# The two S5 recurrences of a four-layer trunk in a written order on all engines

## The chip, the cores and the metric

The kernel runs on one core of a Trainium2 chip. Its time is the device time of one execution in microseconds; several executions give a median. A profile is one execution, taken by the hardware profiler. The core has five engines with instruction queues of their own, which run side by side and meet through semaphores: PE (TensorE, matrix products and transposes; PEld is its weight load), DVE (VectorE), ACT (ScalarE), POOL (GpSimd) and SP (SyncE, which here only issues DMAs). Each of them takes its instructions in the order of its queue, so that an instruction that waits holds up all that stand behind it.

## The reference, cut to what matters

A trunk of four layers on 512 positions of width 1024. Layers 0 and 3 mix by an S5 recurrence, layer 1 by gated linear attention, layer 2 by differential attention; each is followed by a SwiGLU FFN. The change touches the S5 layers only:

```python
def s5_mixer(h, lam_re, lam_im, log_dt, b_re, b_im, c_re, c_im, d_skip, w_glu):   # h = rmsnorm(x, norm_mix[layer])
    dt = jnp.exp(log_dt)[:, None]
    ab = exp((lam_re + 1j * lam_im) * dt)             # 64 groups of 64 states (written as re, im in the reference)
    bb = (ab - 1) / lam * b                           # 64 groups, 64 states, 16 inputs
    for chunk in chunks(h, 64):                       # u: positions x 64 groups x 16
        bu = einsum('bcgh,gph->bcgp', u, bb)
        s = associative_scan(s_t = ab * s_(t-1) + bu_t), started from the chunk before
        y = real(einsum('bcgp,ghp->bcgh', s, c))
    y = y + d_skip * h
    z = gelu(y)
    a, b = split(z @ w_glu, 2)
    return a * sigmoid(b)
...
x = x + mix;  h = rmsnorm(x, norm_ffn[layer]);  x = x + swiglu_ffn(h, w_gate_up[layer], w_down[layer])
```

## The kernel before, in words

**The whole.** `Trunk.run` goes through `s5_first` (layer 0), an FFN, `gla`, an FFN, `diff`, an FFN, `s5_second` (layer 3), an FFN and the last norm. Products of weights are made in three passes over a high and a low half of each operand (`mm3`, lines 368 to 372): ScalarE casts the high half (L346), VectorE subtracts it for the low half (L350). Weights arrive in `wst` tiles (three buffers) and are split into `whl` tiles (five buffers).

**The order of work.** By default a list scheduler orders each engine's instructions by priorities and its own costs. `self.hand(engines)` ends the part before and opens one in which the named engines take their instructions as they are written (`hand_all` for all five; `hand()` goes back to the scheduler). The first blocks of each FFN, the attention and parts of `gla` are written like that; before the change, both S5 layers are left to the scheduler. `issue_after` puts the instructions of a block behind one of another place, on that one's engine.

**One S5 layer.** Four positions are taken together: a step of the recurrence goes over 128 blocks of four positions. `s5_pipe` (L1266) works through eight steps `kk`, each for 8 of the 64 groups (128 channels):

- `up`: four transposes turn `hu` (the normed input) into U, one of four buffers of `room` (L1290, copied by ScalarE L1303; for the first four steps of the second layer VectorE scales them, L1299).
- `states`: 8 products with the input operator `in` into two PSUM banks `V` (L1311); VectorE multiplies by cosine and sine `cs` (L1313 to L1316) and adds the pairs (L1318, L1319), on GpSimd in layer 0, on VectorE in layer 3.
- `scans`: two scans with the decays `r4` (L1328, L1330) and four products that turn back, into `prods` (L1329, L1331 to L1333).
- `outputs`: 20 products with the operators `map` and `out` into `y` (L1340, L1342), then Gelu on ScalarE (L1344).
- `turned`: four transposes `zp` (L1353), and the high (L488) and low (L489) halves of `zT`.
- `glu`: 12 three-pass products of 512 columns with `w_glu`'s second half, over steps into four banks `acc`, which `s5_glu` reads through Tanh (L1548).

A turn of the loop at L1374 writes `states(kk)`, `scans(kk-1)`, `up(kk+1)`, the `steps` hook, `outputs(kk-2)`, `turned(kk-2)` and `glu(kk-3)`. The two pairs of `mods` and `prods` hold four of the five `whl` buffers while the recurrence runs, so one is left for the halves of `w_glu`.

**Where the operators come from.** In layer 0 they are made while it runs. `s5_small` makes the parameters, `s5_x` the input operators X of eight blocks (parts `one` and `two`, by `cross`, L1017 to L1019, on VectorE), `s5_xt` and `s5_inm` turn them into `in` (L1143, four ScalarE copies L1153), `s5_q` makes the output operators Q (base copies L1075, `cross` on GpSimd), `s5_out_pads` and `s5_b_pads` lay them out by DMA on SP, `s5_rows` and `s5_map` make `map` (L1110, L1120, a trip through DRAM). `s5_phases_first` makes cosines and sines of a step: rough turns (L987 to L992, banks `tp`), their fraction (L994 to L996), a clip on VectorE (L998) and three ScalarE operations (L999 to L1001), where sine and Gelu need different function tables; then the decays (L1003, L1004). The `steps` hook makes them for `kk + 1`. The input is normed by `s5_in` over `normed` (L470 to L484): squares on ScalarE, the power on GpSimd, scaling and the norm's weight on ScalarE and GpSimd for two of four quarters and on VectorE for the others.

In layer 3 the operators were made under earlier FFNs and lie in DRAM; `steps` loads them one step ahead (L1505, L1513), with the decays' copy (L1516) on ScalarE.

Of the kernel before, what the change touches and what calls it, by code (L numbers as in the profile page):

```python
# [11 lines left out]
F32 = mybir.dt.float32  # L12
# [256 lines left out]
class Trunk:  # L269
# [558 lines left out]
    def sincos(self, pool, sn, cs, r, n, tag):  # L828
# [6 lines left out]
        with self.tc.high_priority(offset=60):  # L835
            nc.scalar.activation(sn, r, AF.Sin)
            nc.scalar.activation(cs, a[:], AF.Sin, scale=-1.0, bias=self.halfpi[:])


    def s5_small(self, pool):  # L840
# [6 lines left out]
        nc.scalar.activation(warm[:], self.halfpi[:], AF.Sin)  # L847
        self.magic = cp.tile([P, 1], F32, name="magic")
# [5 lines left out]
        if True:  # L854
# [5 lines left out]
            draw = p.tile([16, P], F32, name="draw")  # L860
            nc.sync.dma_start(draw[:], i["s5_d"].rearrange("l (k p) -> (l k) p", p=P))
# [6 lines left out]
            nc.tensor.transpose(ps[:, 3, :16], draw[:], self.ident[:16, :16])  # L868
# [10 lines left out]
            v.tensor_copy(self.dcol[:], ps[:, 3, :16])  # L879
# [58 lines left out]
        p = Slices(self.wp.tile([P, 2048], F32, tag="whl", name="params2", bufs=5))  # L938
        self.s5_rows_of_phases(p, pool, keep["fhi"], keep["flo"], keep["f"])
# [3 lines left out]
    def s5_rows_of_phases(self, p, cp, fhi, flo, f):  # L943
# [4 lines left out]
        v = nc.vector  # L948
        part = p.tile([P, 96], F32, name="rowparts").rearrange("p (k z b) -> p k z b", z=3, b=4)
# [8 lines left out]
        v.tensor_tensor(lo, lo, rest, op=ALU.subtract)  # L958
# [19 lines left out]
    def s5_phases_first(self, pool, kk, cs, r4):  # L978


        nc = self.nc
        mm = nc.tensor.matmul
        flat = lambda y: y[:].rearrange("p a b -> p (a b)")
        row = self.frow[:, kk]
        fine, rest = (self.counts[:, z].rearrange("p a b -> p (a b)") for z in range(2))
        rough = flat(self.tp("rough"))
        mm(rough, row, fine, start=True, stop=False)  # L987
        mm(rough, row, rest, start=False, stop=True)
        k = pool.tile([P, 512], F32, tag="turns", name="turns")
        nc.scalar.activation(k[:], rough, AF.Identity, bias=self.magic[:])  # L990
        kr = pool.tile([P, 512], F32R, tag="turnsr", name="turnsr")
        nc.scalar.activation(kr[:], k[:], AF.Identity, bias=self.mmagic[:])  # L992
        g = flat(self.tp("angle"))
        mm(g, row, fine, start=True, stop=False)  # L994
        mm(g, self.nident[:], kr[:], start=False, stop=False)
        mm(g, row, rest, start=False, stop=True)  # L996
        ca = k[:]
        nc.vector.tensor_scalar(ca, g, -0.5, 0.5, op0=ALU.max, op1=ALU.min)  # L998
        nc.scalar.activation(cs[:, 1], ca, AF.Sin, scale=self.two_pi)  # L999
        nc.scalar.activation(ca, ca, AF.Abs)  # L1000
        nc.scalar.activation(cs[:, 0], ca, AF.Sin, scale=-self.two_pi, bias=self.halfpi[:])  # L1001
        r4 = r4.rearrange("p (b m) -> p b m", m=P)
        nc.scalar.copy(r4, self.k5["r4"][:, 4 * kk : 4 * kk + 4].unsqueeze(2).broadcast_to([P, 4, P]))  # L1003
        nc.gpsimd.memset(r4[:, :, 0:1], 0.0)  # L1004
# [28 lines left out]
    def s5_x(self, eng, pool, L, b0, nb, bb, bufs=1):  # L1033
# [4 lines left out]
        def one():  # L1038
            f(0, 0, X[:, 0, :, 0], bb[:, 0], bb[:, 1], ALU.subtract)
# [96 lines left out]

    def s5_xt(self, X, z, b0):
# [11 lines left out]
    def s5_inm(self, dst, ps):  # L1149
        d = dst.rearrange("p (b n) -> p b n", n=P)  # L1150
        for g in range(2):
            r = slice(g * 64, (g + 1) * 64)
            self.nc.scalar.copy(d[r, :, r], ps[r, :, r])  # L1153
# [105 lines left out]
    def s5_in(self, p, l, xin, pool, aside=False):  # L1259
        g = self.gain(self.i["norm_mix"][l])  # L1260
# [932 lines left out]
```

## Time and profile before

| | |
|---|---|
| median of three runs | 2357.49 us (2357.08 to 2360.3) |
| the profiled execution | 2366.1 us, its span 2364.4 us |
| mean granted TensorE clock | 0.977 |
| first scan products (L1313) of layer 0 | 48.6 us from the start |
| gates of layer 0 read (L1548) | from 201.7 us |
| first scan products of layer 3 | 1846.8 us |
| gates of layer 3 read | from 1939.6 us |

The profile gives busy times by engine, the waits with what ended them, and a timeline of instructions (start, duration, engine, line, operation, tiles, times merged; in brackets the idle time before it and its releaser). Durations of pipelined instructions overlap a little, so that the distance from one start to the next is the time one costs. The PEclk column is the granted clock of TensorE as a share of full speed.

### The profile page before, as it was taken

The page shows a single profiled execution, that of the slowest core. Times are in us where ns is not written, and L with a number is a line of the kernel's source. Part 1 is how long each engine was busy: PE and PEld are TensorE (multiplying, and loading weights), DVE is VectorE, ACT ScalarE, POOL GpSimd, SP SyncE. Part 2 cuts the span into 40 slices and gives each one's busy share as a digit, 9 for nine tenths or more (in the row PEclk, how much of TensorE's full clock was granted, in tenths as well). Part 3 has the DMA queues.
Part 4 walks back from the last instruction along what each step waited for, and adds up shares of the span by engine and source line. Part 5 has one row for each costly group of instructions (what it writes and reads, how often), then busy time and mean ns, then how long its engine had stood idle before and what let it go on. Part 6 is the DMA issues. An engine that isn't in the chain of part 4 may idle for free. (4 is left out here: it accounts for less than half of the span.)

```text
span 2364.4 us, 37216 instructions
## 1 busy us (share of the span) xinstructions
PE 2245.8 (95%) x14847; PEld 1985.6 (84%) x14847; DVE 1586.0 (67%) x2416; ACT 1119.2 (47%) x1790; POOL 332.3 (14%) x417
## 2 busy tenths in 40 slices
PE   4799989999999999999999998999999799999997
PEld 3577888898977789898987787989999688989996
DVE  7765587876833468786753566886856864967674
ACT  3454454554552346555544575653534233634442
POOL 3330123324000011111001231111000100101000
PEclk9699999999999999999999999999999899999999
DMA  4114676676332268576344564895742545766631
GB/s 111 32 39 142 160 186 155 165 178 156 86 104 72 79 144 212 146 181 177 108 140 116 115 134 122 209 240 127 187 98 81 121 130 151 176 175 157 162 77 67
DMA packets 291719, 320.17 MB, mean 135 GB/s; under 512 B 68005, under 2 KB 231097, under 8 KB 291290
## 3 DMA queue, kind: packets, MB, share of 16 engines
q1 hardware_dynamic: 229434, 236.57, 33.4%
q0 software_dynamic: 62112, 81.22, 18.7%
q8 instruction: 117, 1.92, 0.3%
q14 instruction: 56, 0.46, 0.1%
HBM read 285.88 MB, written 16.65 MB: 128 GB/s over the span
## 5 line engine op out<-in xcount | busy, mean ns | idle before, releaser
L350 DVE TENSOR_TENSOR whl<-wst,whl 128x1024 fp32r<-128x1024 f32 x272 | 332.1, 1223 | 310.2 <-ACT whl L346 309.6
L346 ACT CAST whl<-wst 128x1024 fp32r<-128x1024 f32 x272 | 285.2, 1050 | 383.2 <-PE acc L372 265.5
L535 PE MATMUL a<-side,whl 128*128 128x256 f32 x3168 | 388.7, 280 | 9.0 <-ACT whl L346 5.9
L535 PEld LDWEIGHTS a<-side,whl 128*128 128x128 f32 x3168 | 375.9, 191 | 11.0 <-ACT whl L346 7.1
L370 PE MATMUL acc<-whl,act 128*128 128x512 f32 x704 | 278.2, 395 | 3.0 <-DVE g L580 3.0
L371 PE MATMUL acc<-whl,act 128*128 128x512 f32 x704 | 275.0, 391 | 0.0
L372 PE MATMUL acc<-whl,act 128*128 128x512 f32 x704 | 274.7, 390 | 0.0
L535 PE MATMUL c<-side,whl 128*128 128x256 f32 x2112 | 255.8, 278 | 4.3 <-DVE whl L350 4.3
L535 PEld LDWEIGHTS c<-side,whl 128*128 128x128 f32 x2112 | 248.6, 189 | 4.7 <-DVE whl L350 4.7
L350 DVE TENSOR_TENSOR whl<-slot,whl 128x1024 fp32r<-128x1024 f32 x105 | 127.9, 1223 | 66.4 <-ACT whl L346 65.9
L370 PEld LDWEIGHTS acc<-whl,act 128*128 128x128 f32 x704 | 132.1, 188 | 33.2 <-DVE g L580 4.2
L372 PEld LDWEIGHTS acc<-whl,act 128*128 128x128 f32 x704 | 132.2, 188 | 28.0
L371 PEld LDWEIGHTS acc<-whl,act 128*128 128x128 f32 x704 | 132.2, 188 | 25.9 <-issue 0.2
L370 PE MATMUL acc<-whl,hT 128*128 128x512 f32 x352 | 143.4, 407 | 2.1 <-DVE ro L1918 1.5
L346 ACT CAST whl<-slot 128x1024 fp32r<-128x1024 f32 x105 | 110.0, 1052 | 73.9 <-PE acc L372 28.2
L371 PE MATMUL acc<-whl,hT 128*128 128x512 f32 x352 | 138.4, 393 | 1.0 <-DVE whl L350 1.0
L372 PE MATMUL acc<-whl,hT 128*128 128x512 f32 x352 | 138.5, 394 | 0.0
L535 PE MATMUL a<-sides,whl 128*128 128x256 f32 x1056 | 134.0, 283 | 1.6 <-DVE x L518 1.6
L535 PE MATMUL d<-sides,whl 128*128 128x256 f32 x1056 | 133.5, 283 | 1.3 <-ACT whl L346 1.3
L535 PEld LDWEIGHTS a<-sides,whl 128*128 128x128 f32 x1056 | 129.4, 191 | 2.7 <-issue 2.0
L535 PEld LDWEIGHTS d<-sides,whl 128*128 128x128 f32 x1056 | 128.9, 191 | 2.0 <-ACT whl L346 1.9
L571 POOL DMA_DIRECT2D wst<-in_ffn_w_gate_up_dram x44 | 56.8, 1290 | 445.7 <-DMA wst<-in_ffn_w_gate_up_dram 257.1
(442 smaller groups left out, 3994.7 us busy)
## 6 DMA issues: line engine op xcount, KB each, us to landing
wst<-in_ffn_w_gate_up_dram SPq DMA_DIRECT2D x88, 512.0 KB, 4.5
wst<-in_ffn_w_down_dram SPq DMA_DIRECT2D x88, 512.0 KB, 4.6
slot<-in_ffn_w_gate_up_dram SPq DMA_DIRECT2D x69, 512.0 KB, 5.4
wst<-in_ffn_w_gate_up_dram POOLq DMA_DIRECT2D x44, 512.0 KB, 6.3
halves<-in_ffn_w_gate_up_dram SPq DMA_DIRECT2D x42, 512.0 KB, 6.2
wst<-in_s_w_glu_dram SPq DMA_DIRECT2D x32, 512.0 KB, 3.9
wst<-in_gla_w_in_dram SPq DMA_DIRECT2D x24, 512.0 KB, 3.7
wst<-in_diff_w_qkv_dram SPq DMA_DIRECT2D x24, 512.0 KB, 3.8
```

The source lines that it names most:

```text
L346: self.last["high"] = self.nc.scalar.copy(hl[:, 0], w[:])
L350: self.last["low"] = self.nc.vector.tensor_tensor(hl[:, 1], w[:], hl[:, 0].bitcast(F32), op=ALU.subtract)
L370: mm(out, lh, rh, start=first, stop=False)
L371: mm(out, lh, rl, start=False, stop=False)
L372: self.last["mm"] = mm(out, ll, rh, start=False, stop=last)
L535: mm(o, hl[:, x, k, c], side[:, y, k], start=first and not (j or k or n), stop=k == 3 and n == 2, skip_group_check=True,)
L571: nc.gpsimd.dma_start(w[:], left.quarter(*plus, b), accum_op=ALU.add)
```

## The change

Both recurrences are put between `hand_all()` and `hand()`. The loop of `s5_pipe` is written anew: `states` is cut into `products` (TensorE) and the VectorE part, the scans from the turns, `turned` from its low half `rest`; the outputs follow one step behind the states, and `glu` two. The sums are on VectorE in both layers. In layer 0 the `in` operators are made two steps ahead in two buffers by two copies each, the phases two steps in each of the turns 0 to 2, in the `acc` banks that `glu` takes later; the norm's weight is multiplied into B (`s5_x` with `gain`) and, for the skip path, into `dcol`, and the input is normed on ScalarE alone. `cs` is kept for five steps. In layer 3 the loads run two steps ahead.

The diff, cut to its core:

```diff
@@ s5_small
+            nc.sync.dma_start(draw[16:], i["norm_mix"][0].rearrange("(k p) -> k p", p=P))
...
+            v.tensor_tensor(self.dcol[:, :8], gcol[:, :8], gcol[:, 16:], op=ALU.mult)
@@ s5_phases_first: three parts; turns in normp's "h" and "hh", banks by self.acc
+        def rough(): ...   # two products, two Identity on ScalarE
+        def angle(): ...   # three products
+        def table(): ...   # clip on VectorE, Sin, Abs, Sin on ScalarE
+        return rough, angle, table
+    def s5_decays(self, L, kk, r4): ...   # one ScalarE copy, one GpSimd memset
@@ s5_x
+            if gain is not None:
+                g = gain[:, b0 : b0 + nb].unsqueeze(1).broadcast_to([P, 2, nb, 16])
+                eng.tensor_tensor(bb[:], bb[:], g, op=ALU.mult)
@@ s5_in
+        def scaled(t):
+            nc.scalar.mul(hu[:, :, 3 - t], gr(xin[:, t]), rs[t][:])
         for t in range(NT):
-            self.normed(xin[:, t], g, hu[:, :, 3 - t], pool, aside and t < 2)
+            nc.scalar.activation(junk[:], xin[:, t], AF.Square, scale=1.0 / 32.0, accum_out=ms[:])
+            nc.scalar.activation(ms[:], ms[:], AF.Identity, bias=self.eps[:])
+            rs.append(self.rsqrt(ms[:], 1, 0.0))
+            if t:
+                scaled(t - 1)
+        scaled(NT - 1)
@@ s5_pipe
+        self.hand_all()
...
-        up(0)
-        for kk in range(11):
-            if kk < 8:
-                states(kk)
-            if 1 <= kk < 9:
-                scans(kk - 1)
-            if kk + 1 < 8:
-                up(kk + 1)
-            if steps:
-                steps(kk)
-            if 2 <= kk < 10:
-                outputs(kk - 2)
-            ...
+        before(up, products)
+        for kk in range(10):
+            hook("first", kk)
+            if kk < 8:
+                states(kk)
+            if kk + 2 < 8:
+                up(kk + 2)
+            if 1 <= kk < 9:
+                outputs(kk - 1)
+            hook("behind outputs", kk)
+            if kk + 1 < 8:
+                products(kk + 1)
+            if 1 <= kk < 9:
+                turned(kk - 1)
+            if kk < 8:
+                scans(kk)
+            hook("behind scans", kk)
+            if kk < 8:
+                turns(kk, 0)
+            if 1 <= kk < 9:
+                rest(kk - 1)
+            if kk < 8:
+                turns(kk, 1)
+            if kk % 2 == 0:
+                if kk < 8:
+                    stage[kk // 2] = self.staged(self.wb_src(wg, kk, D), 2, 512)
+                if kk >= 2:
+                    hls[kk // 2 - 1] = self.halves(stage[kk // 2 - 1], 2, 512)
+            if kk >= 2:
+                glu(kk - 2)
+            hook("last", kk)
+        self.hand()
@@ s5_first
+            src = i["norm_mix"][0].rearrange("(b g c) -> g b c", g=2, c=16)
+            for g in range(2):
+                nc.sync.dma_start(gain[g * 64 : (g + 1) * 64], src[g].partition_broadcast(64))
             nc.sync.dma_start(xin[:], i["x"][0].rearrange("(p t) c -> p t c", t=NT))
+            raw[1] = self.s5_loads(p, 0, 8, 8, 2)
+            self.hand(mybir.EngineType.PE, mybir.EngineType.Activation)
+            with self.tc.issue_after(self.last_sine.ins):
+                hu = self.s5_in(scr, xin)
+                ps = self.s5_qt(raw[0][1])
+            self.s5_rows_of_phases(p)
+            new_x(0); X[0][1]()
+            with self.tc.issue_after(self.last_row.ins):
+                X[0][2](); self.s5_b_pads(bp, X[0][0])
+                Q[0] = self.s5_q(nc.vector, p, 0, 0, 8, 2) ...
+            room = four buffers, and z in the gain tile's second half ("wide") and in "R"; cs4 + cs1: five phases
+            before: out_pads(0, 1), up(0), up(1), rough(0), ins(0), new_x(1), angle(0), rough(1), table(0),
+                    X[1] one, decays(0), products(0), maps(0), angle(1), table(1), ins(1)
+            first: rough(2kk+2), rough(2kk+3) for kk < 3; decays(kk+1)
+            behind outputs: X[1] two (kk 0); angle of both (kk < 3); out_pads(kk+1)
+            behind scans: table(2kk+2), table(2kk+3) (kk < 2) or one (kk 2); ins(kk+2)
+            last, kk even: table(7) (kk 2); b_pads, Q of the next eight blocks on GpSimd; X one of the eight after
+            last, kk odd: maps of the next eight blocks; X two
@@ s5_second
+            before: left.finish(), up(0), products(0), up(1), zeros of outs on GpSimd, out_of(0)
+            behind outputs: out_of(kk+1); into(kk+2), decays(kk+2)
```

More of the change, by code (lines that the diff above doesn't have):

```diff
@@ L1471, in s5_first @@
[L1471 to L1473 removed]
+                        X[h + 2][2]()
+            hooks = {"first": first, "behind outputs": behind_outputs, "behind scans": behind_scans, "last": last}
+            accs = self.s5_pipe(0, hu, zT, True, room, get, before, hooks)
         self.x = self.xp.tile([P, NT, D], F32, tag="x", name="x")
```

359 lines of the change are left out of this document (217 added, 142 removed).

## The prediction

> **What bounds the kernel now.** I read the page first, then the busy time of each engine over the two recurrences, then the waits inside the first one, then both timelines.
>
> ```profile
> span 2364.4 us, 37216 instructions
> PE 2245.8 (95%) x14847; PEld 1985.6 (84%) x14847; DVE 1586.0 (67%) x2416; ACT 1119.2 (47%) x1790; POOL 332.3 (14%) x417
> ...
> core 0: us, PE busy (x) PEld busy (x) DVE busy (x) ACT busy (x) POOL busy (x), PEclk, DMA share, GB/s
> 48.63:205.00 156.37, 134.53 (x1034) 107.99 (x1034) 102.82 (x134) 78.17 (x129) 51.47 (x45) 0.84 0.25 59
> 1844.30:1883.20 38.90, 27.99 (x170) 26.40 (x171) 37.81 (x55) 9.38 (x15) 2.03 (x8) 0.78 0.59 136
> 1883.20:1942.00 58.80, 58.30 (x428) 53.25 (x428) 45.14 (x62) 18.35 (x28) 0.11 (x1) 1.00 0.49 138
> ```
>
> TensorE bounds the kernel as a whole; only where it waits or runs at a reduced clock can this change win. The first recurrence takes 156 us for eight steps with no engine full (VectorE 103, ScalarE 78) and a clock of 0.84. The second has two halves: 39 us in which VectorE is full (37.8 of 38.9) and TensorE is not, then 59 us in which TensorE has no gap. So the first has much to give, the second little, and its full half can only be damaged.
>
> ```profile
> POOL mods L1318 <- DVE mods L1315: 31.6, 4, 11.3
> DVE turns L998 <- PE angle L996: 16.5, 6, 8.2
> DVE prods L1329 <- PE y L1342: 14.3, 4, 5.0
> ```
>
> These waits (us, times, longest) between 40 and 205 us say why: the scheduler's order interleaves operators, phases and outputs, so that VectorE waits 8.2 us for one angle, GpSimd 11.3 us for a product of VectorE, and VectorE again 5.0 us for outputs that still read `prods`. None of these engines is full, so an order that puts the phases ahead and the outputs a step earlier can close such gaps.
>
> **The prelude.**
>
> ```profile
> 16.10 1.06 ACT L470 ACTIVATE sq<-xin 128x1024 f32<-128x1024 f32 x1 [8.82 <-DMA xin<-in_x_dram]
> 17.15 0.24 ACT L836 ACTIVATE params<-params 128x64 f32<-128x64 f32 x1
> 19.89 2.34 DVE L904 TENSOR_TENSOR params<-params 128x64 f32<-128x64 f32 x1
> 26.81 0.22 ACT L956 CAST params<-params 128x32 fp32r<-128x32 f32 x1 [5.56 <-DVE params L954]
> 33.67 1.29 DVE L481 SCALAR_TENSOR_TENSOR scr<-xin,rs,gain 128x1024 f32<-128x1024 f32 x1 [3.17 <-POOL rs L459]
> 48.63 0.69 DVE L1313 TENSOR_TENSOR mods<-V,cs 128x512 f32<-128x512 f32 x1 [4.18 <-PE V L1311]
> ...
> xin<-in_x_dram SPq DMA_DIRECT2D x1, 2048.0 KB, 8.1
> bb<-in_s_b_re_dram SPq DMA_DIRECT2D x4, 64.0 KB, 2.7
> ```
>
> The norm now lies on ScalarE alone. Ahead of `xin` on SP stand two gain loads in 64-byte pieces, 4096 in all, where four operator loads (2560 pieces) stood: The 1536 more pieces cost between nothing and 4 us (one `bb`, 1024 pieces, lands in 2.7, much of it latency); I take 1.7, so `xin` lands at 17.8, not 16.1. Four squares (1.06 and the reading of the sum, 1.15), eps copies (0.2, as the short L836) and scalings (1.13, taken as long as a square) and one wait of 0.8 for the last power give 28.5; the two halves that VectorE normalised until 35 (L481) thereby come earlier. Behind them in ScalarE's written order come the cast of L956 (26.8 before), the row copies, four `Q` copies, two `up` copies and `rough`: 35.2; the eight transposes between cast and copies are in this. Then follow the first clip, the first sines and the first clip of step 1. The sines of L836 no longer stand behind the square, and the 2.34 us beside GpSimd's gain multiplication goes. `Q[0]` moves to VectorE, 6 operations, 4 us. I get L1313 at 41.6 instead of 48.6: a gain of 7.
>
> **The first recurrence, step by step.**
>
> ```profile
> L1342 PE MATMUL y<-scr,prods 128*128 128x128 f32 x256 | 39.2, 301 | 0.0
> L1319 POOL TENSOR_TENSOR mods<-mods 128x512 f32<-128x512 f32 x8 | 14.6, 1820 | 2.4 <-DVE mods L1316 2.4
> L1019 POOL TENSOR_TENSOR Q<-Q,dq 128x512 f32<-128x512 f32 x8 | 12.2, 1524 | 0.3
> L1328 DVE TENSOR_TENSOR_SCAN mods<-cs,mods 128x512 f32<-128x512 f32 x8 | 12.6, 1573 | 1.2 <-POOL mods L1318 1.2
> L488 ACT CAST zT<-zp 128x512 fp32r<-128x512 f32 x8 | 8.8, 1096 | 9.0 <-PE zp L1353 9.0
> L489 DVE TENSOR_TENSOR zT<-zp,zT 128x512 fp32r<-128x512 f32 x8 | 8.6, 1077 | 0.9 <-ACT zT L488 0.9
> L1344 ACT ACT_TABLE_LOAD x5 | 6.4, 1283 | 0.1
> L990 ACT ACTIVATE turns<-rough,magic 128x512 f32<-128x512 f32 x7 | 4.8, 687 | 2.5 <-PE rough L988 2.2
> L1001 ACT ACTIVATE cs<-turns,halfpi 128x512 f32<-128x512 f32 x8 | 5.8, 723 | 0.1
> L350 DVE TENSOR_TENSOR whl<-wst,whl 128x1024 fp32r<-128x1024 f32 x8 | 9.7, 1220 | 11.0 <-ACT whl L346 11.0
> ...
> 1846.75 0.68 DVE L1313 TENSOR_TENSOR mods<-V,cs 128x512 f32<-128x512 f32 x1
> 1850.33 1.22 DVE L1328 TENSOR_TENSOR_SCAN mods<-cs,mods 128x512 f32<-128x512 f32 x1
> 1856.15 0.69 DVE L1329 TENSOR_TENSOR prods<-mods,cs 128x508 f32<-128x508 f32 x1
> 1858.55 0.69 DVE L1313 TENSOR_TENSOR mods<-V,cs 128x512 f32<-128x512 f32 x1
> ```
>
> VectorE's own row is read from the second recurrence, where the sums lie on it already: four products and two sums 3.6 us (1846.75 to 1850.33), two scans 2.3, four products 2.4 (1856.15 to 1858.55). With the low half of `zT` at 1.0 a step is 9.3. Added per pair of steps, from the kernel's smaller operations at 0.2 to 0.5 us each: an operator (one 3.1 with the gain multiplication, two 1.5), map rows 0.4, low weight half 1.15; and a clip of 0.6 for each phase. The sums thus cost VectorE 1.2 us a step and free 16 operations of up to 1.8 us on GpSimd; what it keeps is six operations of `Q`, at most 1.5 us each and 6.5 us together, three times.
>
> ScalarE: two tables in each of steps 0 to 2 (two operations like L990, 1.4, and three of 0.6 to 0.7 like L1001, 2.0), and one switch to Gelu and back in steps 1 and 2 (1.28 each way; nine loads before, L1344's five and four more, five now).
>
> My chain goes by whichever engine's written list ends last, VectorE and ScalarE being nearly level at first. Step 0, VectorE 3.6 + 1.5 + 2.3 + 1.2 + 2.4 + 3.1 = 14.1. Step 1, ScalarE-bound, 14.3. Step 2, ScalarE 18.5 (rough 2.8, decays, `up`, Gelu with load 3.0, cast 1.1, first table with load 3.3, `inm` 1.2, high 1.05, second table 2.0, `Q` 1.1) with its wait for the transposes, then VectorE's `X`: 22.5. From step 3 on there is one loop. TensorE does outputs 4.4, the next products 1.8, the transposes 0.5; then cast, `rest`, the second half of the turns. In an even step VectorE's low weight half (`hls`) comes last, and `glu`, written behind it, stands in front of the next outputs on TensorE's queue. So an even step takes about 11.5 and the odd one after it starts its outputs 3.2 us late (`glu` 2.75, `up` 0.45) and takes about 13.5: VectorE, through with scans and half the turns 7.2 us into the step, waits for the cast until some 10.5. With `Q` and map copies: 12.4, 10.5, 15.2, 11.7, 11.9. Tail from the last turns: outputs, Gelu, transposes, cast, `rest`, low, two `glu` = 14.8. Sum: 41.6 + 14.1 + 14.3 + 22.5 + 61.7 + 14.8 = 169.
>
> What this leaves out has no row of its own: GpSimd's `Q` beside VectorE (L1328's mean is 1.57 us, against 1.22 where GpSimd rests) between 0 and 13 us, I take 3, since in steps 1 and 5 VectorE waits for the cast anyway; and TensorE at a reduced clock between 0 and 25 us, I take 8, as in the early steps its gaps are long. So 180.
>
> ```profile
> 201.68 2.67 ACT L1548 ACTIVATE gate<-acc 128x512 f32<-128x512 f32 x4 [1.82 <-PE acc L372]
> ...
> 1893.65 1.95 PE L1311 MATMUL V<-room,in 128*128 128x128 f32 x16
> 1895.87 0.39 PE L1340 MATMUL y<-out,room 128*128 128x128 f32 x2
> 1900.26 0.47 PE L370 MATMUL acc<-whl,zT 128*128 128x512 f32 x1
> 1901.94 0.59 ACT L488 CAST zT<-zp 128x512 fp32r<-128x512 f32 x1 [0.74 <-PE zp L1353]
> 1903.59 1.95 PE L1311 MATMUL V<-room,in 128*128 128x128 f32 x16
> ...
> 1939.58 2.52 ACT L1548 ACTIVATE gate<-acc 128x512 f32<-128x512 f32 x4 [2.09 <-issue]
> ```
>
> The gates read the sums to 204.3; TensorE then has the next product. Gain of the first recurrence: 204 - 180 = 24.
>
> **The second recurrence.** A full step of TensorE is 9.94 us (1893.65 to 1903.59): products, `up` 2.2, outputs 4.4, `glu` and transposes 3.3. The scheduler fills the wait from outputs to cast (1.7 us behind the outputs' end) with `glu`. Written, `glu` is last: outputs, products, transposes, cast, `rest`, second turns, low, `glu`. By the same loop, with the cast and `rest` at 0.6: even steps 11.2, odd 12.7, a pair 23.9 against 19.9. The early part gains, since outputs come a step sooner: 1866 for the second outputs. From 1856 the outputs start at 1866, 1880, 1890, 1904, 1914, 1927, 1936, the last `glu` ends at 1950 against 1942: 8 lost, 9 with one cooled stretch.
>
> **At nothing:** loads two steps ahead, the zeroing of `out` and the smaller SP list: a step's DMAs fill under half of it. `dcol` times the weight is one small operation. The next gain load waits for `wide` (read to the last transposes) and holds SP's later weight loads; cover is two `glu`; without it 3 us.
>
> **Sum.** On the profile's own time (2366.1, span 2364.4, 1.7 around it): -24 + 9 = -15, giving 2351. The median of the runs is 2357.5, 8.6 below the profiled execution; the same difference gives **2342.5**.
>
> [...]
>
> ```profile
> 1845.13 2.58 PE L1311 MATMUL V<-room,in 128*128 128x128 f32 x16 [1.13 <-DMA cs<-cs]
> 1871.78 1.12 PE L1353 MATMUL zp<-ident,room 128*128 128x128 f32 x4 [6.63 <-ACT room L1344]
> ```
>
> After a gap of 6.6 us the transposes take 1.12 us, and sixteen products 2.58 where 1893.65 shows 1.95. My chain puts a gap of 3.8 us before `glu` in each even step. [...]
>
> **Rivals.**
>
> *Gaps cool TensorE (slower).* Place: the wait of `glu` for the low half, and of outputs for turns, in both recurrences. If most steps run at a clock under about 0.8, outputs grow from 4.4 to 7 and `glu` from 2.8 to 4: about 4 us a step. First: 7 steps and the tail, 169 + 3 + 28 = 200, gain 4. Second: 9 + 5 x 2 = 19 lost; net 15 slower, 2372; half of it, 2364. For it: 0.78 in the thin half. Against: 1883 to 1942 at 1.00. [...]
>
> *VectorE sets the pace.* If casts arrive before VectorE needs them, the first ends at 41.6 + 92.5 (the sum of its steps) + 14.8 = 149, 55 gained; a middle of 40 is likelier, and the second breaks even: 2317. For it: VectorE full in 1844 to 1883. Against: `glu` is written behind the low half.
>
> *It doesn't do what it says.* The long steps 0 to 2 on ScalarE eat the prelude's gain, the first wins 10 and the second loses 9: 2357.
>
> **Chances.** Forecast 0.48, VectorE's pace 0.17, no net effect 0.14, cooled 0.21. The measurement of this kernel tells about 0.2%, 4.7 us, from no change. Faster 0.48 + 0.17 and little more: 0.65; same 0.14; slower 0.21. The forecast's own range is 2330 to 2352 (reduced clock 0 to 20 us, `Q` 0 to 5). Reaching to the middle of VectorE's case and of the cooled one gives 2318 to 2366.
>
> **What would show it.** Right: L1313 first near 42 us, no sums on GpSimd, the first gates near 180, the gates of the second about 8 us later after its start, PEld waits for the low half in even steps. Wrong: clock under 0.8 past step 3, or the second recurrence at 20 us a pair.

## The result: 2366.4 us where 2342.5 was predicted, and the profile after

The changed kernel takes 2366.43 us (median of 20 runs, 2361.91 to 2371.71), the kernel before 2359.98 (20 runs beside them, 2355.76 to 2368.5): a ratio of 1.0029 (95% interval 1.0020 to 1.0038). It is slower, by a little more than can be told from no change, and the forecast of 2342.5 and its range missed. The profiled execution of the changed kernel took 2364.8 us.

Its page begins:

```profile
span 2363.1 us, 37145 instructions
PE 2241.5 (95%) x14847; PEld 1981.6 (84%) x14847; DVE 1591.0 (67%) x2439; ACT 1115.0 (47%) x1776; POOL 300.8 (13%) x395
```

Only GpSimd's sum moved visibly (332.3 to 300.8): the sums are gone from it. The busy time by stretch says more: the first recurrence up to the end of its gate reads, then the second in two parts from the first product with `Rt` (L1351):

```profile
core 0: us, PE busy (x) PEld busy (x) DVE busy (x) ACT busy (x) POOL busy (x), PEclk, DMA share, GB/s
46.11:190.60 144.49, 119.73 (x970) 99.27 (x965) 107.31 (x153) 68.85 (x108) 27.26 (x26) 0.87 0.31 77
1827.20:1866.00 38.80, 30.02 (x190) 27.08 (x191) 36.49 (x53) 9.62 (x15) 1.79 (x5) 0.87 0.63 163
1866.00:1942.30 76.30, 65.97 (x414) 58.32 (x414) 45.52 (x63) 18.41 (x29) 0.31 (x3) 0.89 0.36 101
```

The first takes 144 us instead of 156 at about the same clock (0.87, 0.84 before). The second's later part, 59 us without a gap at 1.00 before, now takes 76 with 10 us of gaps and a clock of 0.89. Two milestones sum it up, and they are used for every run below: the first read of the first gates (L1701) came at 187.6 us instead of 201.7, and the second recurrence, from the first product with `Rt` to its first gate read, took 111.2 us (1827.2 to 1938.4) instead of 95.2 (1844.3 to 1939.6): 14 us won, 16 lost.

The waits name what was lost: the first four rows are from the first recurrence, the last three from the second (us in all, times, longest).

```profile
DVE zT L1421 <- ACT zT L1417: 21.8, 5, 6.9
PE acc L370 <- ACT whl L346: 11.9, 4, 5.6
DVE turns L1011 <- PE angle L1007: 4.7, 3, 3.6
PE acc L371 <- DVE whl L350: 4.0, 4, 2.1
...
DVE zT L1421 <- ACT zT L1417: 24.6, 7, 6.7
PE acc L370 <- ACT whl L346: 6.5, 4, 1.6
PE acc L371 <- DVE whl L350: 5.6, 4, 1.6
```

The wait of the clip for the angle fell (16.5 us before), and GpSimd's wait for state products (31.6) went with the sums. In their place `glu` (L370 to L372 on TensorE) waits in both recurrences for two things, four times each: the high half of its weights (L346, ScalarE) and then the low half (L350, VectorE). The timeline of one even step of the second recurrence shows how that looks (start, us; idle time and its releaser in brackets):

```profile
1855.04 0.60 PE L1416 MATMUL zp<-ident,room 128*128 128x128 f32 x4
1855.68 0.58 ACT L1417 CAST zT<-zp 128x512 fp32r<-128x512 f32 x1 [1.12 <-PE zp L1416]
1856.16 1.05 ACT L346 CAST whl<-wst 128x1024 fp32r<-128x1024 f32 x1
1857.26 0.50 PE L370 MATMUL acc<-whl,zT 128*128 128x512 f32 x1 [1.62 <-ACT whl L346]
1857.50 0.68 DVE L1392 TENSOR_TENSOR prods<-mods,cs 128x508 f32<-128x508 f32 x1
1858.10 1.22 DVE L350 TENSOR_TENSOR whl<-wst,whl 128x1024 fp32r<-128x1024 f32 x1
1859.37 0.69 PE L371 MATMUL acc<-whl,zT 128*128 128x512 f32 x1 [1.60 <-DVE whl L350]
1859.86 0.63 PE L372 MATMUL acc<-whl,zT 128*128 128x512 f32 x1
...
1862.42 0.63 PE L372 MATMUL acc<-whl,zT 128*128 128x512 f32 x1
1862.85 0.43 PE L370 MATMUL acc<-whl,zT 128*128 128x512 f32 x1
1863.12 0.40 PE L371 MATMUL acc<-whl,zT 128*128 128x512 f32 x1
...
1864.02 0.39 PE L1399 MATMUL y<-out,room 128*128 128x128 f32 x2
```

Read it from the top: the cast, the high half, one product; the last turns, the low half, the next product. Both halves were written at the end of the step, so each stands behind the last work of its engine. Then eight products of `glu` start 0.43 us apart instead of 0.23: TensorE has fallen to half pace (PEclk 0.52 from 1859.37 to 1862.85), and comes back at 1862.85. The next outputs start at 1864.02, 16.1 us after those of the step before (1847.97).

### The profile page after: what moved, and what is told of

It reads as the page before. It is cut to its first block, busy times and chain, and to the rows that moved or that the text cites. A ratio compares the mean times of both kernels' runs of the same rounds, so it can differ in the third digit from the quotient of the medians.

```text
span 2363.1 us, 37145 instructions
## 1 busy us (share of the span) xinstructions
PE 2241.5 (95%) x14847; PEld 1981.6 (84%) x14847; DVE 1591.0 (67%) x2439; ACT 1115.0 (47%) x1776; POOL 300.8 (13%) x395
## 5 line engine op out<-in xcount | busy, mean ns | idle before, releaser
L350 DVE TENSOR_TENSOR whl<-wst,whl 128x1024 fp32r<-128x1024 f32 x272 | 331.6, 1223 | 296.2 <-ACT whl L346 295.6
L346 ACT CAST whl<-wst 128x1024 fp32r<-128x1024 f32 x272 | 284.9, 1051 | 373.8 <-PE acc L372 261.3
L370 PE MATMUL acc<-whl,act 128*128 128x512 f32 x704 | 278.4, 396 | 3.1 <-DVE g L580 2.2
L372 PE MATMUL acc<-whl,act 128*128 128x512 f32 x704 | 274.7, 390 | 0.0
L350 DVE TENSOR_TENSOR whl<-slot,whl 128x1024 fp32r<-128x1024 f32 x105 | 127.9, 1222 | 65.7 <-ACT whl L346 65.2
L370 PEld LDWEIGHTS acc<-whl,act 128*128 128x128 f32 x704 | 132.1, 188 | 34.2 <-DVE g L580 4.0
L372 PEld LDWEIGHTS acc<-whl,act 128*128 128x128 f32 x704 | 132.1, 188 | 27.9
L346 ACT CAST whl<-slot 128x1024 fp32r<-128x1024 f32 x105 | 110.0, 1052 | 73.8 <-PE acc L372 28.1
L370 PE MATMUL acc<-whl,hT 128*128 128x512 f32 x352 | 142.8, 406 | 2.1 <-DVE ro L2071 1.5
L372 PE MATMUL acc<-whl,hT 128*128 128x512 f32 x352 | 138.1, 392 | 0.0
L370 PE MATMUL acc<-whl,zT 128*128 128x512 f32 x256 | 108.5, 424 | 18.4 <-ACT whl L346 18.4
```

The lines of the kernel that those rows point to most:

```text
L346: self.last["high"] = self.nc.scalar.copy(hl[:, 0], w[:])
L350: self.last["low"] = self.nc.vector.tensor_tensor(hl[:, 1], w[:], hl[:, 0].bitcast(F32), op=ALU.subtract)
L370: mm(out, lh, rh, start=first, stop=False)
L372: self.last["mm"] = mm(out, ll, rh, start=False, stop=last)
```

## Experiments

Each kernel was run beside the kernel before. Gates and second recurrence are the two milestones, from the profile.

| run | median us | ratio (95% interval) | first gates | second |
|---|---|---|---|---|
| before, three profiles | 2359.98 | 1 | 201.7, 194.7, 201.1 | 95.2, 95.1, 95.1 |
| changed, two profiles | 2366.43 | 1.0029 (1.0020 to 1.0038) | 187.6, 187.5 | 111.2, 111.4 |
| e1 second left to the scheduler | 2349.32 | 0.9959 (0.9944 to 0.9974) | 188.8 | 95.1 |
| e2 halves early | 2333.94 | 0.9893 (0.9876 to 0.9910) | 176.9 | 92.4 |
| e3 and `rest` last | 2335.44 | 0.9896 (0.9879 to 0.9912) | 176.9 | 90.7 |
| e4 26 idle products | 2364.83 | 1.0021 (1.0010 to 1.0033) | 188.3 | 113.2 |
| e5 17 idle products | 2357.94 | 0.9990 (0.9977 to 1.0003) | 188.7 | 104.0 |
| e6 e2, sums on GpSimd | 2344.60 | 0.9934 (0.9912 to 0.9955) | 185.6 | 93.2 |
| e7 e2, prelude reordered | 2339.62 | 0.9906 (0.9884 to 0.9928) | 177.2 | 93.5 |
| e8 e2, `glu` ahead at the end | 2339.05 | 0.9906 (0.9891 to 0.9921) | 175.3 | 91.2 |
| e9 e2, next splits held | 2322.70 | 0.9830 (0.9813 to 0.9847) | 167.5 | 88.6 |
| e10 e8 and e9 | 2325.61 | 0.9846 (0.9830 to 0.9862) | 169.6 | 89.2 |
| e11 only the high half early | 2371.96 | 1.0046 (1.0033 to 1.0059) | 192.5 | 112.7 |
| e12 e9, warm prelude | 2318.00 | 0.9832 (0.9819 to 0.9845) | 162.5 | 88.7 |

The expectations were written with 112.6 for the changed second, up to the second row of its gate reads; up to the first it is 111.2. The theory at the outset: the written order of the second costs the 16 us, since `glu` waits there for its weight halves and TensorE cools in the gap. The rivals: the loop from outputs through cast and `rest` to the next outputs sets the step; or what is lost lies elsewhere.

**e1: the second recurrence as before.** `s5_second` and its `s5_pipe` are those of the kernel before, the first is as changed.

> The first recurrence as in the changed kernel (written), the second with the code of the kernel before (left to the scheduler). Measured from the first product with Rt (before 1844.3, changed 1827.2) to the start of the last gate (1939.6 and 1939.8), the second took 95.3 us before and 112.6 changed. Theory (the written order of the second is what costs 16 to 17 us, the first keeps its 14): 95 us for the second, ratio to before 0.993, 2343 us. Rival (the second is slower because of what it meets, for instance transfers that are now earlier, and not because of its order): 105 to 113 us for the second, ratio 0.999 to 1.003. Rival (the first gains nothing by itself, the shift came from elsewhere): ratio 1.000 with the second at 95.

The second is back at 95.1 us, and the kernel is 17 us faster than the changed one: the second as rewritten costs all that it lost. Its loads went back together with its order; the runs below show which two lines of that order matter. The ratio to before fell short of 0.993; the last part of this section says why.

**e2, e3, e11: where the halves stand.**

```diff
 e2:         states(kk)
+            if kk % 2 == 0 and kk >= 2:
+                hls[kk // 2 - 1] = self.halves(stage[kk // 2 - 1], 2, 512)
...
             if kk % 2 == 0: ...
-                if kk >= 2:
-                    hls[kk // 2 - 1] = self.halves(stage[kk // 2 - 1], 2, 512)
 e3: as e2, and rest(kk - 1) behind turns(kk, 1)
 e11: only self.high behind the states, self.low at the old place
```

> The changed kernel with one edit in both recurrences: the split of the next two blocks of GLU weights (high half on ScalarE, low on VectorE) is written behind the states of the even step instead of at its end. Theory (glu waits for both halves, and the gap cools TensorE): in the second the two waits of glu go, the clock stands at 1.00, a pair of steps takes 20 to 21 us instead of 26, so 95 to 97 us from Rt to the last gate, and the first gains another 4 to 6: ratio 0.990 to 0.992 (2337 to 2342 us). Rival (the loop outputs, Gelu, transposes, cast, rest, second turns, outputs sets the step, wherever the halves stand): a pair stays at 24 or more, the second at 107 or more, ratio 0.998 or more.

> As the run with the halves behind the states, and besides the low half of zT (rest) is written behind the second half of the turns instead of ahead of it, so that the next outputs do not wait for the cast of the last step. Theory (waits for the halves and the clock): equal to the run with the halves alone within 3 us, since TensorE has no gap there any more. Rival (the loop through the cast sets the step): only this run brings the pair to 20 us, 5 to 12 us faster than the run with the halves alone.

> The changed kernel, and only the high weight half (ScalarE) is written behind the states of the even step; the low half (VectorE) stays at the end. Theory (the low half behind the second turns ends the wait of glu, the high half only the part before it): glu begins one product earlier and then waits for the same low half, 0 to 3 us over all, ratio 1.001 to 1.003. Rival (the high half behind the cast of zT on ScalarE is what delays the low half): the low half comes earlier too, a pair of steps shorter by 1 to 2 us, ratio 0.995 to 1.000.

With two lines moved, the loss becomes a gain of 1.1%. In e2's timeline `glu` follows the transposes at once, and in its windows TensorE is busy 10.00 of 10.00 us at a clock of 1.00 from 1840 to 1890:

```profile
1861.86 1.95 PE L1363 MATMUL V<-room,in 128*128 128x128 f32 x16
1863.65 0.60 PE L1416 MATMUL zp<-ident,room 128*128 128x128 f32 x4
1864.00 0.48 PE L370 MATMUL acc<-whl,zT 128*128 128x512 f32 x1
1864.32 0.40 PE L371 MATMUL acc<-whl,zT 128*128 128x512 f32 x1
```

A pair of outputs takes 19.8 us (1847.47 to 1867.26), about what the theory said, and the second 92.4, 3 us less than left to the scheduler. The first recurrence gained 10.7 us, about twice what was expected. The loop through the cast is not what sets the step: e3, which takes `rest` out of it, is within 0.1% of e2 (its second 90.7 against 92.4). With the high half alone early (e11) nothing is won; the product behind it waits 3.49 us in one piece for the same low half, and from there TensorE runs at half pace as before, its products 0.43 us apart up to 1870.86:

```profile
1863.47 0.48 PE L370 MATMUL acc<-whl,zT 128*128 128x512 f32 x1
...
1867.44 0.64 PE L371 MATMUL acc<-whl,zT 128*128 128x512 f32 x1 [3.49 <-DVE whl L350]
```

So the low half ends the wait, and at the same moment as in the changed kernel (32.1 and 32.2 us behind the first product with `Rt`). e11's second is near the changed one's (112.7), and it came out slower than expected because of its first, 5 us behind the changed one at the gates; why, no run was made to show.

**e4, e5: the clock by itself.** Idle products fill the wait, in the second only; nothing else is moved, and their results are not used.

```diff
+            if left and kk % 2 == 0 and kk >= 2:
+                warm = self.tp("warm")
+                for n in range(26):   # e5: 17
+                    mm(warm[:, n % 4], U0[:, bs(n % 4)], self.ident[:], start=True, stop=True)
             if kk >= 2:
                 glu(kk - 2)
```

> The changed kernel with 26 idle products of 128x128 (about 3.2 us at 0.12) put ahead of glu in the even steps of the second recurrence alone; their results are not used, the order of the rest is as changed. They fill the time in which glu waits for its two weight halves. Theory (the reduced clock is a part of the loss of its own): glu then runs its 12 products at full clock, 2.5 to 3 us less in each of four even steps, the second at 101 to 104 us instead of 112.6, ratio 0.995 to 0.999. Rival (the wait alone costs, the clock comes back by itself): second within 2 us of 112.6, or up to 4 us slower, ratio 1.002 to 1.005.

> As the first run with idle products, but 17 of them instead of 26: one took 0.22 us there (two passes), so 26 lasted 5.9 us and outran the wait of 3.9 us that they were to fill; 17 last 3.8. Theory (the reduced clock is a loss of its own): glu begins when it does in the changed kernel and takes 2.75 us instead of 4.3 in each of four even steps: 5 to 7 us less, the second at 106 to 108 us from the first product with Rt to the last gate (112.6 changed), ratio to before 1.000. Rival (the wait alone costs): within 2 us of the changed kernel, ratio 1.002 to 1.004.

e4 was mis-sized. Its fillers lasted 5.97 us and held `glu` up:

```profile
1856.12 5.97 PE L1471 MATMUL warm<-ident,hu 128*128 128x128 f32 x52
1861.84 0.48 PE L370 MATMUL acc<-whl,zT 128*128 128x512 f32 x1
```

In e5 they end with the wait:

```profile
1857.12 3.96 PE L1471 MATMUL warm<-ident,hu 128*128 128x128 f32 x34
1860.83 0.48 PE L370 MATMUL acc<-whl,zT 128*128 128x512 f32 x1
1861.15 0.39 PE L371 MATMUL acc<-whl,zT 128*128 128x512 f32 x1
...
1864.08 0.39 PE L1399 MATMUL y<-out,room 128*128 128x128 f32 x2
```

`glu` still waits for its weights, but the products behind the first take 2.5 us (1861.15 to `up` at 1863.65) instead of 4.2 (1859.37 to 1863.59), and the second falls from 111.2 to 104.0 though TensorE does more. So of the 16 us, 7 are the clock. The other 9 are the waits less a gain: without the waits (e2) the written order takes 92.4, 3 us less than the scheduler's, so the waits themselves cost 11.6 (104.0 to 92.4).

**e6: the sums back on GpSimd**, on top of e2, in the first recurrence (`e = v if L else nc.gpsimd`).

> The kernel with the halves behind the states (2333.9 us, first gates at 176.9 us), and in the first recurrence the two sums of the states back on GpSimd. Theory (the sums stand in the chain from states to scans, where GpSimd takes 1.8 us for what VectorE does in 0.6): 1 to 2.5 us a step longer, first gates at 185 to 197, ratio 0.993 to 0.998. Rival (VectorE, full between 120 and 160 us there, sets the pace, and 1.2 us a step less on it is time won): first gates at 169 to 174, ratio 0.986 to 0.988.

The theory holds: 8.8 us later at the first gates. GpSimd takes 1.27 and 1.64 us for the two sums and waits for VectorE ahead of them, and VectorE's scans wait in turn, as the third line shows for the first step:

```profile
L1374 POOL TENSOR_TENSOR mods<-mods 128x512 f32<-128x512 f32 x8 | 13.1, 1640 | 0.0
L1373 POOL TENSOR_TENSOR mods<-mods 128x512 f32<-128x512 f32 x8 | 10.2, 1272 | 11.0 <-DVE mods L1370 11.0
...
54.17 2.27 DVE L1378 TENSOR_TENSOR_SCAN mods<-r,mods 128x512 f32<-128x512 f32 x1 [3.94 <-POOL mods L1373]
```

**e7, e12: the prelude.** e7 (on e2) writes `rough` of step 1, both angles and the first products ahead of the map; e12 (on e9) keeps the order and puts idle products on TensorE between 24 and 31 us.

```diff
 e7, before(): rough(0), ins(0), new_x(1),
-    angle(0), rough(1), table(0), X[1] one, decays(0), products(0), maps(0), angle(1), table(1), ins(1)
+    rough(1), angle(0), table(0), products(0), angle(1), X[1] one, decays(0), maps(0), table(1), ins(1)
 e12, s5_rows_of_phases:
+        filler(9)     # idle products on hu, ready at about 24 us
         for q in range(2):
             ... four transposes
+            filler(4)
```

> The kernel with the halves behind the states, and ahead of the first step the phases of steps 0 and 1 (rough and angle) and the first products are written in front of the operators and the map on TensorE, which the angle of step 1 stood behind. Theory (the prelude fell short by 4.5 us of the predicted 41.6 since the first state product is written behind the second clip, and that behind the map's transposes): first state product at 42 to 44 us instead of 45.6, first gates 2 to 3 us earlier at 174 to 175, ratio 0.988. Rival (ScalarE, which bounds steps 1 and 2, eats it): first gates within 1 us of 176.9, ratio 0.989 to 0.990.

> The fastest version so far (halves behind the states, next splits behind the last cast: 2322.7 us, first state product at 46.0 us, first gates at 167.5), and in the prelude idle products on TensorE, 9 ahead of the transposes of the phase rows (about 24 to 28 us) and 4 behind each group of them; their results are not used. There TensorE stood idle for 18 us and then takes 2.3 us for eight transposes and 3.5 for sixteen products that take 1.95 at full clock. Theory (the prelude missed 41.6 because TensorE, written in one order, goes through rough, transposes, angles and products cold): the first state product at 41 to 43 us, first gates 3 to 4 us earlier, ratio 0.981. Rival (ScalarE's casts and copies and VectorE's Q set it): first state product at 45 to 46.5, ratio 0.983.

The reordering failed: the first state product came at 46.3, in e2 at 45.6. e12 shows the cause, a slow TensorE. In the changed kernel it enters the prelude after 18 us of rest and is slow for 15 us (of the lines below, the 64 by 64 transposes take 1.7 and the sixteen products 1.8 times what they take in e12; the PEclk column reads 1.00 there, so the pace is read from the products), so that its one written list of products sets the pace. Two gaps of 0.7 us stand at the start of these 15 us; behind them, from 31.20 to 43.25 us, the profile has it busy for 11.94 of 12.05 us:

```profile
27.83 1.02 PE L970 MATMUL frow<-ident,params 128*12 128x128 f32 x4 [18.29 <-DVE params L965]
31.20 2.34 PE L1342 MATMUL up<-ident,scr 128*128 128x128 f32 x8 [0.67 <-ACT frow L971]
34.62 1.97 PE L1167 MATMUL xps<-ident,X 64*64 64x64 f32 x32
39.54 3.78 PE L1363 MATMUL V<-room,inm 128*128 128x128 f32 x16
```

With idle products for 4.2 us ahead and 1.1 us in each of the two gaps (e12), the same transposes take 1.15 and the products 2.05, and the first state product comes at 40.7 instead of 46:

```profile
33.13 1.15 PE L1175 MATMUL xps<-ident,X 64*64 64x64 f32 x32
36.05 2.05 PE L1371 MATMUL V<-room,inm 128*128 128x128 f32 x16
...
40.73 0.68 DVE L1376 TENSOR_TENSOR mods<-V,cs 128x512 f32<-128x512 f32 x1
```

The first gates follow by 5.0 us (162.5). Whether the products ahead or those in the gaps did it was not tried apart. The ratio does not show it (0.9832, as e9); the profiled spans differ by 2.2 us, so whether it lasts to the end is open.

**e8, e9, e10: the end of each recurrence.** In e2 the scheduler puts weight splits of the product that follows ahead of the last Gelu on ScalarE's queue. In the changed kernel the last Gelu (176.75 us) has no such split right ahead of it, so this came with e2's edit. One of the splits waits for its transfer, and the Gelu and the transposes behind it wait too:

```profile
168.50 1.04 ACT L346 CAST whl<-wst 128x1024 fp32r<-128x1024 f32 x1 [8.41 <-DMA wst<-in_s_w_glu_dram]
169.45 0.59 ACT L1403 ACTIVATE z<-y 128x512 f32<-128x512 f32 x1
170.09 1.11 PE L1416 MATMUL zp<-ident,z 128*128 128x128 f32 x4 [6.97 <-ACT z L1403]
```

```diff
 e8:  as e2; at kk == 8, glu(6) ahead of turned(7)
 e9:  as e2; in s5_glu, the product behind the first gates is written under
+     issue_after(the last cast of zT), issue_after(the last rest)
 e10: both
```

> The kernel with the halves behind the states (first gates at 176.9 us, last gates at 1908.4), and in the last but one step glu of block 6 is written ahead of the last four transposes on TensorE, so that it fills the wait for the last Gelu (7.0 us in the first recurrence, 3.0 in the second). Theory (TensorE cools in that wait and runs both last glu behind it): first gates 2 to 4 us earlier, last gates another 2 to 3: ratio 0.986 to 0.988. Rival (the chain from the last Gelu through cast and low half to the last glu sets the end, whatever lies in front): gates within 1 us, ratio 0.989 to 0.990.

> The kernel with the halves behind the states, and the splits of the next product's weights (high halves on ScalarE, low on VectorE) held behind the last cast and the last low half of zT. There the scheduler puts three such high halves in front of the last Gelu on ScalarE's queue, and one of them waits 8.4 us for its transfer in the first recurrence (4.4 in the second). Theory (the last Gelu stands behind a weight split that waits for a transfer): first gates at 170 to 172 us instead of 176.9, last gates 3 us earlier still: ratio 0.985 to 0.987. Rival (the product behind the gates waits for the same transfer anyway): gates earlier, but the first combination of gate and sum stays within 2 us of 198.6, ratio 0.989 to 0.990.

> Both edits together, the halves behind the states besides: glu of block 6 ahead of the last transposes, and the next product's weight splits behind the last cast. Theory: the two waits at the end of each recurrence go, gates at 169 to 171 us and last gates 9 to 11 us earlier than with the halves alone, ratio 0.984 to 0.986. Rival (the two overlap, one alone does it all): equal to the better of the two within 2 us.

e9 gained 9.4 us at the first gates and 3.8 in the second, more than expected; the first combination of gate and sum (L1704) came at 188.2 instead of 198.6, so the rival, that the product behind waits for that transfer anyway, falls. The Gelu now comes 8 us earlier and the split waits behind it:

```profile
161.47 0.60 ACT L1403 ACTIVATE z<-y 128x512 f32<-128x512 f32 x1 [5.93 <-PE y L1401]
162.81 1.08 ACT L1417 CAST zT<-zp 128x512 fp32r<-128x512 f32 x1 [0.75 <-PE zp L1416]
166.52 1.05 ACT L346 CAST whl<-wst 128x1024 fp32r<-128x1024 f32 x1 [0.82 <-DMA wst<-in_s_w_glu_dram]
167.48 2.05 ACT L1701 ACTIVATE gate<-acc 128x512 f32<-128x512 f32 x4
```

e8 treats the symptom only, and the time does not show it; e10 is no better than e9. e9 and e12 beat both kernels, by 1.7% against before.

**The spread of the first recurrence.** Both kernels were profiled again; the kernel before twice.

> The kernel before, profiled once more. In the profiles the changed kernel was 14.2 us ahead behind the first recurrence and 17.1 us at the start of the second, though nothing between them differs; the profiled before stood 6 us over its median. Theory (the 3 us between are spread of the before profile, which lies in the stretch between the recurrences): this profile ends that stretch 3 to 6 us earlier, while its first and second recurrence take the same 202 and 95 us within 1. Rival (the changed start of the middle is a real gain): the same times as in the first profile within 1 us.

> The kernel before, a third profile. Two profiles of it read the first gates at 201.7 and 194.7 us (times 2366.1 and 2357.5). Theory (its first recurrence itself varies by 7 us from run to run, by the clock that TensorE gets in its gaps): the first gates again lie with the time, at 194 to 196 if the run is near 2357 and 200 to 203 if it is near 2366. Rival (the first profile was a single outlier of another kind): gates at 194.7 within 1 us whatever the time.

> The changed kernel, profiled once more (first: 2364.8 us, first gates at 187.6, second recurrence 111.2 us from the first product with Rt to the first gate read). Theory (it is 7 us ahead of a middling run of the kernel before behind the first recurrence and loses 16 in the second): gates at 186 to 193, second at 110 to 113. Rival (the 187.6 was a lucky run): gates at 194 or later.

The second profile of the kernel before took 2357.5 us and the third 2362.6, and their first gate reads stood at

```profile
194.68 2.67 ACT L1548 ACTIVATE gate<-acc 128x512 f32<-128x512 f32 x4 [1.85 <-PE acc L372]
```

```profile
201.09 2.70 ACT L1548 ACTIVATE gate<-acc 128x512 f32<-128x512 f32 x4 [1.85 <-PE acc L372]
```

against 201.68 in the first (2366.1). The same program takes 7 us more or less in its first recurrence, with a mean granted clock from 48 to 195 us of 0.90 in the shorter case and 0.83 in the two longer ones. The expectation put the spread between the recurrences; from the first gates to the product with `Rt` it is 1642.7, 1640.5 and 1640.0 us, so 2 us lie there and 7 in the first recurrence. Over all the runs this stretch, whose code is the same or nearly so, took from 1635.2 (e9) to 1645.6 us (e3), so that the end of one profile does not tell a few us. The changed kernel's two profiles agree in the first (187.6 and 187.5) and differ by 3.7 us behind it (1639.6 and 1636.0). So the change gains 14 us where the kernel before runs long and 7 where it runs short, and loses 16: 2 to 9 us slower, which holds the 6.5 between the medians. Why the longer case occurs in one run and not in another, the traces do not say.

## Why the prediction was wrong

**What bounds.** Right: the first recurrence had time to give, the second's late part could only be damaged, and it was.

**The prelude: predicted 41.6, measured 46.1; a gain of 2.5 instead of 7.** The steps up to `rough` came out right in sum (`xin` had landed by 17.5 against 17.8, `rough`'s copy ended at 35.4 against 35.2), partly by luck: the norm ended at 27.2 instead of 28.5, and what follows on ScalarE took longer by as much. The step that failed is what "then follow the first clip, the first sines and the first clip of step 1" took: taken as 6.4 us, it took 10.7, since TensorE's list behind it, at the slow pace (sixteen products in 3.78 us, 2.05 in e12), was not costed. With idle products ahead of it and in its gaps the same list brought the first product at 40.7 (e12).

**The first recurrence: predicted 180 for the end of the last `glu`, measured about 190.** Distances between first state products, predicted with no reduced clock, and measured in the changed kernel and in e2:

| | steps 0 to 6 | last step and tail |
|---|---|---|
| predicted | 14.1, 14.3, 22.5, 12.4, 10.5, 15.2, 11.7 | 26.7 to the end of `glu` |
| changed | 14.7, 15.8, 24.8, 16.6, 10.4, 18.7, 11.0 | 29.5 to the first gate read |
| e2 | 14.7, 16.3, 21.8, 16.6, 10.3, 14.1, 10.3 | 27.2 to the first gate read |

The seven steps sum to 100.7 predicted and 112.0 measured. The 11 us added cover that in sum, but not as they were split, 3 for GpSimd's `Q` beside VectorE and 8 for the clock. Step 3 is 4.2 us over and stays so in e2: five operations of VectorE took 4.4 us longer there than in other steps, while GpSimd made `Q` (the scan below takes 1.22 elsewhere, the product 0.66):

```profile
103.89 1.47 POOL L1036 TENSOR_TENSOR Q<-Q,pw 128x512 f32<-128x512 f32 x1 [22.03 <-ACT Q L1098]
105.83 2.07 DVE L1377 TENSOR_TENSOR_SCAN mods<-r,mods 128x512 f32<-128x512 f32 x1
109.99 1.47 DVE L1388 TENSOR_TENSOR prods<-mods,cs 128x508 f32<-128x508 f32 x1
```

Steps 2 and 5 shrink by 3.0 and 4.6 us in e2, so what they were over belongs to the late halves. The last gate read begins some 2 us after the first, so the tail was 5 us too short: the last outputs began 13.6 us into step 7 instead of 11.9, then `glu` waited 2.00 us for its high half and 0.65 for its low one, and went on at half pace, 0.43 us a product, until 186.75. From e2 to e9 the first gate comes another 9.4 us sooner, but that wait was e2's own. The late halves with the clock behind them were thus worth about 20 us here (187.6 to 167.5 in e9), of which the chain had only a part. The sums cost VectorE 0.6 us each, as said, and e6 shows that their move was right.

**The second recurrence: predicted +9, measured +16.** The mechanism was named: `glu`, written last, stands behind the low half. The 8 us for the wait were right: with TensorE back at full pace behind the wait (e5, products 0.23 us apart) the loss is 8.8, and from the second outputs on the outputs start 14.5, 9.9, 13.7, 9.4, 13.2 and 8.6 us apart, predicted 14, 10, 14, 10, 13 and 9. The mis-sized term is "one cooled stretch", taken as 1 us, measured as 7. What the chain also missed is that the high half, on ScalarE behind the cast, is a second wait; with the low half late anyway it costs nothing (e11).

**What gaps did to TensorE's pace.** In e11 a gap of 3.49 us was followed by 3.4 us of products 0.43 us apart (1867.44 to 1870.86), then 0.23. In the changed kernel two gaps of 1.62 and 1.60 us with one product between them did the same, for 3.5 us (1859.37 to 1862.85). In the prelude the slow pace lasted longer: TensorE, busy for 11.94 of 12.05 us, kept it to the end of them (sixteen products in 3.78 us, 2.05 in e12). The forecast left such gaps to a rival. The trace of the kernel before had shown slow transposes behind a gap of 6.63 us in the second recurrence (four in 1.12 us, 0.60 at 1881.43), and no gap between 2.93 and 6.63 us there; the forecast's own chain made one in every even step.

**The rivals.** The cooled rival came nearest: its half, 2364, is 2 us from the result, and its loss for the second (19) is nearer than the forecast's 9. Part of that is luck: it let the first recurrence gain only 4 us, where 7 to 14 were measured. It had a chance of 0.21, though the chain already held a gap of 3.8 us in a place that it names, the wait of `glu` for the low half. "VectorE sets the pace" and "no net effect" did not come about; the 92.5 us that the first of them gives VectorE's steps is not worked out there, and VectorE was busy for 107 of the 144 us.

**The sum.** On the profile's own time the prediction was 2351 against 2364.8: 10 us too little in the first recurrence's time, 7 in the second's, and 3 the other way between them. The other 10 are the step to the median: 8.6 us were taken off because the profiled execution of before lay so far above it. 7 of these lay in the first recurrence, the very stretch that the change replaces (194.7 against 201.7), and could not be carried over; the changed kernel's profile is 1.6 below its own median.

**What was to show it.** Right: no sums on GpSimd, PEld waits for the low half in even steps. Wrong: L1313 near 42, the gates near 180, 8 us in the second. The sign named for a cooled TensorE, a clock under 0.8 past step 3, did not show either: by stretches of 20 us from 100 us on it stood at 0.83 to 0.96, since a mean over 20 us hides 3.5 us at half pace.

## What to carry to other kernels

When an order is written out by hand, go through every queue and ask of each operand when its last producer stands in that queue: two weight splits at the end of a step cost more than the whole reordering brought, and moving two lines turned 0.3% slower into 1.1% faster. A wait like those of TensorE here (3.49 us, or twice 1.6) is to be priced twice, once as the wait and once as the products behind it, at half pace for 3.4 and 3.5 us in the steps shown; idle products that just fill it show which part is which (11.6 us for the waits and 7 for the pace in the second recurrence). Where a profiled execution lies above the median, find out in which stretch before carrying the difference over to a changed kernel.

## What the hardware showed that was not expected

Two idle stretches of 1.6 us with one product of 0.5 us between them slowed TensorE as one of 3.5 did: behind both, products stood 0.43 us apart instead of 0.23, for 3.5 and 3.4 us in the steps shown. In the prelude, after 18 us of rest, TensorE stayed slow through 15 us of work, the last 12 of them without a gap (sixteen products in 3.78 us); with products that nobody reads, 4.2 us ahead of that and 1.1 in each of the two early gaps of 0.7, the sixteen took 2.05 (e12). Whether the gaps kept it slow, or the kind of product there (many fill only 12 rows, or 64 by 64), was not tried. The same operations of VectorE took 0.8 to 1.0 us longer where GpSimd made `Q` at the same time (a scan 2.07 instead of 1.22, a product 1.47 instead of 0.66). One and the same program took two courses through the same recurrence, 7 us apart (first gates at 201.7 and 201.1, and at 194.7), with granted clocks of 0.83 and 0.90.
